# Eight high-half products, then eight low-half products, in a piece of a split-weight matrix product

## The chip, the cores and the metric

One core of one Trainium2 chip runs the whole program. The metric is device time in microseconds, from launch to end; lower is better. The kernel before takes 2523.23 us (median of three runs, 2515.52 to 2528.11).

## What is computed

A decoder trunk of two layers over 256 positions of width 2048. Layer 0 mixes with sliding-window attention and a state-space scan, layer 1 with a recurrent time mixer; each mixer ends in an output projection that is added to x, and each is followed by a squared-ReLU MLP of width 8192. The part that the change touches is the MLP and the two output projections:

```python
def squared_relu_mlp(h, w_up, w_down):
    u = h @ w_up.astype(h.dtype)
    return jnp.square(jax.nn.relu(u)) @ w_down.astype(h.dtype)
...
        x = x + mix.astype(x.dtype)
        h = rms_norm(x, norm_ffn[i])
        x = x + squared_relu_mlp(h, w_up[i], w_down[i]).astype(x.dtype)
```

## The kernel before, in words

Everything is held transposed: 128 channels on the partitions, 256 tokens in the free dimension. A float32 product is made of three products of a shorter format. A weight tile `wt` (128 x 1024, that is eight blocks of 128 x 128) comes in by DMA; ScalarE (ACT) rounds it to `hi` and VectorE (DVE) makes `lo = wt - hi`. The activations are kept the same way, `SA` and `SB`, 16 channel blocks of 512 columns: the first 256 columns are the rounded activations, the other 256 the remainder. For one block TensorE (PE) does `hi` times all 512 columns and `lo` times the first 256. Below, these are called a hi product and a lo product, and the two of one block a pair.

`unit` (line 378) makes one output tile of 128 channels. It goes over two halves h of the 2048 inputs; a half is one tile `wt`, called a piece, with eight pairs. All pairs of a unit add up in one PSUM bank `pu` of 512 columns: the hi product fills the whole bank, the lo product adds to columns 256 to 511. There are two banks `pu` (lines with `pu_119` and `pu_235` in the order below), and three buffers each for `wt`, `hi` and `lo` (126/127, 164/165 and 237/238 for hi/lo).

`mlp` (line 520) runs, four times over: 16 up-units, each followed on ACT and DVE by `eb`, `u`, `uw`, `ut` and the two halves of one block of `SB` (in the second MLP `SA`); then 16 down-units, whose sum is added to x by two DVE adds (`xh<-xh,pu`, later `xT`) before the bank is free again. In the first MLP the last three of the 64 down-units are done elsewhere. `out_proj` (line 1037) is a run of units with the same two adds and, behind them, the next norm's work (`acc`, `SA`). For the first seven tiles of layer 0's output projection the first half is done earlier, so these units have one piece.

The mixers' own projections do not go through `unit`. `feed` (line 431) issues them as three products of 256 columns a block: hi, hi, lo, all into the same 256 columns. That code is not changed. Its rows are called feed below.

In the MLPs and output projections a scheduler sets the order of each engine's instructions by its own estimates; engines then run their queues in that order and wait for semaphores.

Of the kernel before, what the change touches and what calls it, by code (L numbers as in the profile page):

```python
# [295 lines left out]
class Part:  # L296


    def __init__(self, unit, h, src, X=None, n=8, m=P, k0=0, end=16, tiles=None, ready=None, bank=None):
        self.unit, self.key, self.src, self.X, self.n, self.m = unit, unit + (h,), src, X, n, m  # L300
        self.k0, self.end, self.tiles, self.ready, self.bank = k0, end, tiles, ready, bank
# [17 lines left out]
class Trunk:  # L319
# [59 lines left out]
    def unit(self, src, X, h0=0):  # L379
        nc = self.nc  # L380
        ps = self.psu("pu", 2, [P, 512])
        for h in range(h0, 2):
            wt, hi, lo = (self.wp(n, 3, [P, 8 * P], t).rearrange("p (k m) -> p k m", m=P)
                          for n, t in (("wt", F32), ("hi", F32R), ("lo", F32R)))
            nc.sync.dma_start(out=wt, in_=src[:, h * 8:h * 8 + 8, :])
            self.act(hi, wt)
            self.sub(lo, wt, hi.bitcast(F32))
            for kk in range(8):
                k = h * 8 + kk
                self.mm(ps, hi[:, kk, :], X[:, k, :], start=k == 8 * h0, stop=False)  # L390
                self.mm(ps[:, L:], lo[:, kk, :], X[:, k, 0:L], start=False, stop=k == 15)
        return ps

# [661 lines left out]
    def mixer1_in(self, h, SA, SB, scaled, spill, end):  # L1055
# [9 lines left out]
        with tc.tile_pool(name="rh", bufs=1) as rh, tc.tile_pool(name="rht", bufs=1) as rt, \  # L1065
# [10 lines left out]
            def unit(n, j, src, i, m=P, cut=2, bank=None):  # L1076
                s = NK // cut
                return [Part((n, j), q, src[:, q * s:q * s + s, :], (SA, SB)[i not in (0, 3)], s, m, q * s, bank=bank,
                             ready=lambda k: [("mix", i, k)]) for q in range(cut)]

            hidden = [unit("w", 0, ap["w1"], 1, 96), unit("a", 0, ap["a1"], 4, 96),
                      unit("g", 0, ap["g1"][0], 5) + unit("g", 1, ap["g1"][1], 5)]
            parts = [Part(("d", d), q, ap["w_dn0"][3, d][:, q * 8:q * 8 + 8, :], SB, k0=q * 8)
# [665 lines left out]
```

## Time and profile before

| | us |
|---|---|
| median of the runs (3) | 2523.23 |
| lowest, highest | 2515.52, 2528.11 |
| profiled execution, time | 2520.23 |
| profiled execution, span of the trace | 2518.5 |
| PE busy (matmuls) | 2421.8 |
| DVE, ACT, POOL busy | 1768.6, 1315.8, 576.1 |
| granted TensorE clock, mean | 0.983 |

The profiled execution spends 1.7 us outside its span. Units run from about 308 to 1092 us (output projection 0 to 391, MLP 0 behind it) and from about 1754 to the end (output projection 1 to 1802, then MLP 1). In these stretches the granted clock is 1.00. PE's records overlap: the end of a matmul is modelled, so the distance from one start to the next tells the pace, not the duration. In the timeline a row with x2 stands for two instructions of one kind, in turn.

### The profile page before, as it was taken

The numbers are of one execution on the slowest core, as the hardware profiler recorded it, in microseconds if no ns is written. First come the engines' busy times: TensorE is split into PE (matmuls) and PEld (weight loads), VectorE is DVE, ScalarE is ACT, GpSimd is POOL, SyncE is SP. The second block draws the span as 40 slices with busy tenths as digits, with TensorE's granted clock in tenths as the row PEclk, the third lists the DMA queues.
The fourth block names the chain that finished last, engine by engine and source line by source line (L and its number), as shares of the span: only waits on it lengthen the run. The fifth ranks groups of instructions, "written<-read, shape, count | busy, mean of one in ns | idle before, by whom it ended". The sixth has DMA issues, their size and how long they took to land.

```text
span 2518.5 us, 44799 instructions
## 1 busy us (share of the span) xinstructions
PE 2421.8 (96%) x16972; PEld 2165.3 (86%) x16972; DVE 1768.6 (70%) x3330; ACT 1315.8 (52%) x2430; POOL 576.1 (23%) x978
## 2 busy tenths in 40 slices
PE   7999999999999999987998899999999999999999
PEld 7998988888888888877998888888888888888887
DVE  6888776656656656668888888887865665665665
ACT  5455555435435445555555666666653453543543
POOL 3443300000000000036447776774000000000000
PEclk9999999999999999988999899999999999999999
DMA  5333455555555555533544233334555555555554
GB/s 191 139 106 106 142 188 184 187 186 185 187 188 185 185 188 188 201 131 123 175 159 132 84 114 106 112 112 160 186 191 190 188 191 191 188 190 185 187 198 159
DMA packets 130344, 414.67 MB, mean 165 GB/s; under 512 B 23600, under 2 KB 28336, under 8 KB 130128
## 3 DMA queue, kind: packets, MB, share of 16 engines
q1 hardware_dynamic: 128160, 405.91, 47.1%
q0 software_dynamic: 1968, 5.90, 0.6%
q8 instruction: 133, 2.18, 0.3%
q14 instruction: 83, 0.68, 0.1%
HBM read 407.03 MB, written 4.72 MB: 163 GB/s over the span
## 4 chain that ended last, share of the span: by engine, by line
PE 78%; DVE 11%; issue 4%; POOL 3%; ACT 3%; DMA 1%; SPq 0%; POOLq 0%; ACTq 0%; DVEq 0%
PE pu L350 72%; DVE lo L329 2%; PE ps_t L350 1%; PE ps_y L350 1%; POOL xt L329 1%; PE ps_c L350 1%; DVE st L347 1%; ACT hi L326 1%; POOL X L329 1%; PE ps_i L350 1%; PE ps_a L350 1%; DVE AR L329 1%; PE pr L350 0%; PE ps_b L350 0%; ACT ysq L326 0%
## 5 line engine op out<-in xcount | busy, mean ns | idle before, releaser
L329 DVE TENSOR_TENSOR lo<-wt,hi 128x1024 fp32r<-128x1024 f32 (+2 forms) x850 | 898.8, 1060 | 511.7 <-ACT hi L326 494.9
L326 ACT ACTIVATE hi<-wt 128x1024 fp32r<-128x1024 f32 (+2 forms) x945 | 813.6, 873 | 820.3 <-PE pu L350 783.5
L350 PE MATMUL pu<-SA,hi 128*128 128x512 f32 (+2 forms) x4184 | 1154.5, 347 | 10.5 <-ACT SA L326 6.5
L350 PE MATMUL pu<-SB,hi 128*128 128x512 f32 (+2 forms) x3304 | 995.8, 364 | 11.3 <-ACT SB L326 9.2
L350 PE MATMUL pu<-SA,lo 128*128 128x256 f32 (+1 forms) x3168 | 892.1, 282 | 1.5 <-DVE lo L329 1.4
L350 PEld LDWEIGHTS pu<-SA,hi 128*128 128x128 f32 (+1 forms) x4184 | 722.0, 190 | 119.0 <-ACT SA L326 6.5
L350 PE MATMUL pu<-SB,lo 128*128 128x256 f32 x2752 | 773.0, 281 | 0.5 <-DVE lo L329 0.5
L350 PEld LDWEIGHTS pu<-SB,hi 128*128 128x128 f32 (+1 forms) x3304 | 588.1, 190 | 116.5 <-ACT SB L326 10.1
L350 PEld LDWEIGHTS pu<-SA,lo 128*128 128x128 f32 (+1 forms) x3168 | 601.0, 190 | 2.7 <-DVE lo L329 2.1
L350 PEld LDWEIGHTS pu<-SB,lo 128*128 128x128 f32 x2752 | 521.9, 190 | 0.9 <-DVE lo L329 0.7
L1721 POOL DMA_DIRECT2D out<-xT x16 | 8.7, 544 | 699.9 <-DVE xT L329 699.9
L329 POOL TENSOR_TENSOR lo<-wt,hi 128x512 fp32r<-128x512 f32 (+1 forms) x95 | 136.2, 1437 | 127.4 <-ACT hi L326 121.5
L1688 POOL DMA_DIRECT2D xd<-xh x13 | 7.2, 557 | 682.3 <-DVE xh L329 682.3
L329 DVE TENSOR_TENSOR xh<-xh,pu 128x256 f32<-128x256 f32 x164 | 69.1, 421 | 56.5 <-PE pu L350 53.7
L329 DVE TENSOR_TENSOR xT<-xT,pu 128x256 f32<-128x256 f32 x154 | 64.7, 420 | 45.7 <-PE pu L350 43.0
L329 POOL TENSOR_TENSOR xt<-Nb,X 128x60 f32<-128x60 f32 (+14 forms) x240 | 88.4, 368 | 22.9 <-DMA Nb<-dn 6.7
L329 POOL TENSOR_TENSOR X<-X,xt 128x60 f32<-128x60 f32 (+14 forms) x240 | 78.3, 326 | 16.9
L347 DVE SCALAR_TENSOR_TENSOR st<-dx,vec,xh 128x256 f32<-128x256 f32 x80 | 59.9, 763 | 2.9 <-POOL dx L329 2.2
L347 DVE SCALAR_TENSOR_TENSOR uw<-u,rb 128x256 f32<-128x256 f32 x128 | 54.4, 425 | 4.3
L326 ACT ACTIVATE uv<-ps_c,n 64x64 f32<-64x64 f32 x128 | 39.3, 307 | 32.1 <-PE ps_c L350 30.0
L329 DVE TENSOR_TENSOR u<-pu,eb 128x256 f32<-128x256 f32 x128 | 53.4, 417 | 0.0
L326 ACT ACTIVATE ut<-uw 128x256 f32<-128x256 f32 x128 | 51.3, 401 | 2.2 <-DVE uw L347 2.2
(308 smaller groups left out, 2103.2 us busy)
## 6 DMA issues: line engine op xcount, KB each, us to landing
wt<-in_w_up SPq DMA_DIRECT2D x256, 512.0 KB
wt<-in_w_dn SPq DMA_DIRECT2D x256, 512.0 KB
wt<-in_w_in SPq DMA_DIRECT2D x64, 512.0 KB
wt<-in_w_out SPq DMA_DIRECT2D x32, 512.0 KB
wt<-in_w_k SPq DMA_DIRECT2D x32, 512.0 KB
wt<-in_w_v SPq DMA_DIRECT2D x32, 512.0 KB
wt<-in_w_o SPq DMA_DIRECT2D x32, 512.0 KB
wt<-in_w_r SPq DMA_DIRECT2D x26, 512.0 KB
```

What stands on the lines that cost most here:

```text
L326: return self.nc.scalar.activation(out=out, in_=in_, func=func, **kw)
L329: return (eng or self.nc.vector).tensor_tensor(out=out, in0=a, in1=b, op=op)
L347: return self.nc.vector.scalar_tensor_tensor(out=out, in0=a, scalar=s, in1=b, op0=op0, op1=op1)
L350: return self.nc.tensor.matmul(out, lhsT, rhs, start=start, stop=stop)
L1688: spill = lambda d, e=nc.gpsimd: e.dma_start(out=xd[:, d, :], in_=x[d])
L1721: store = lambda d: nc.gpsimd.dma_start(out=ap["out"][:, d, :], in_=x[d])
```

## The change

In each piece, the eight hi products are issued first, then the eight lo products. The same instructions are issued on the same tiles; PSUM accumulation order within a piece changes, and the scheduler sees another program.

```diff
             for kk in range(8):
                 k = h * 8 + kk
                 self.mm(ps, hi[:, kk, :], X[:, k, :], start=k == 8 * h0, stop=False)
+            for kk in range(8):
+                k = h * 8 + kk
                 self.mm(ps[:, L:], lo[:, kk, :], X[:, k, 0:L], start=False, stop=k == 15)
         return ps
```

What it does to the order, at two places. First PE, where the first down-unit of the first MLP follows the last up-unit: before, the end of its second piece (164/165), with the next unit's first products (bank 235, 237/238) behind.

```order
L350 MATMUL pu_119<-SB,hi_164 128x512
L350 MATMUL pu_119<-SB,lo_165 128x256
L350 MATMUL pu_119<-SB,hi_164 128x512
L350 MATMUL pu_119<-SB,lo_165 128x256
L350 MATMUL pu_235<-SB,hi_237 128x512
L350 MATMUL pu_119<-SB,hi_164 128x512
L350 MATMUL pu_119<-SB,lo_165 128x256
L350 MATMUL pu_235<-SB,lo_238 128x256
L350 MATMUL pu_235<-SB,hi_237 128x512
```

The same place after, with the unit's first piece (126/127) ahead of it:

```order
L350 MATMUL pu_119<-SB,hi_126 128x512 x8
L350 MATMUL pu_119<-SB,lo_127 128x256 x8
L350 MATMUL pu_119<-SB,hi_164 128x512 x7
L350 MATMUL pu_235<-SB,hi_237 128x512
L350 MATMUL pu_119<-SB,hi_164 128x512
L350 MATMUL pu_119<-SB,lo_165 128x256 x8
L350 MATMUL pu_235<-SB,hi_237 128x512 x7
L350 MATMUL pu_235<-SB,lo_238 128x256 x8
```

Pairs have become runs of eight. In both programs the scheduler puts the next unit's first hi product ahead of the unit's last one (k = 15); behind that last one stood one lo product of the unit, and now stand eight.

Second DVE, in output projection 0, where units with one piece follow each other: before, the two adds of a unit (`xh<-xh,pu`) stand together.

```order
L329 TENSOR_TENSOR xh<-xh,pu_119 128x256 x2
L329 TENSOR_TENSOR lo_238<-wt_132,hi_237 128x1024
L329 TENSOR_TENSOR acc<-acc,sq 128x256
L347 SCALAR_TENSOR_TENSOR SA<-xh,vec,SA 128x256
L329 TENSOR_TENSOR xh<-xh,pu_235 128x256 x2
L329 TENSOR_TENSOR lo_127<-wt_120,hi_126 128x1024
L329 TENSOR_TENSOR acc<-acc,sq 128x256
L347 SCALAR_TENSOR_TENSOR SA<-xh,vec,SA 128x256
```

After, at the same place:

```order
L329 TENSOR_TENSOR xh<-xh,pu_119 128x256
L329 TENSOR_TENSOR lo_238<-wt_132,hi_237 128x1024
L329 TENSOR_TENSOR acc<-acc,sq 128x256
L347 SCALAR_TENSOR_TENSOR SA<-xh,vec,SA 128x256
L329 TENSOR_TENSOR xh<-xh,pu_119 128x256
L329 TENSOR_TENSOR xh<-xh,pu_235 128x256
L329 TENSOR_TENSOR lo_127<-wt_120,hi_126 128x1024
L329 TENSOR_TENSOR acc<-acc,sq 128x256
```

Between the two adds of a unit there now stand a `lo` and the norm's work of the unit before; the down-units have a `lo` between their two adds in the same way. ACT's order moves the same way (a `hi` one place forward) in output projection 0 and in the last down-units of the first MLP; POOL's and the DMA queue's orders stay as they were.

## Rows read from the trace of the kernel before

**Rows 1.** The page: PE's busy time, and ACT's hi (mean ns, idle before, releaser).

```profile
PE 2421.8 (96%) x16972; PEld 2165.3 (86%) x16972; DVE 1768.6 (70%) x3330; ACT 1315.8 (52%) x2430; POOL 576.1 (23%) x978
...
L326 ACT ACTIVATE hi<-wt 128x1024 fp32r<-128x1024 f32 (+2 forms) x945 | 813.6, 873 | 820.3 <-PE pu L350 783.5
```

**Rows 2.** Groups by line and form, PE: hi products of 512 columns.

```profile
L350 PE MATMUL pu<-SB,hi 128*128 128x512 f32 x2200 | 773.4, 397 | 0.0
...
L350 PE MATMUL pu<-SA,hi 128*128 128x512 f32 x2152 | 757.6, 397 | 1.0 <-DVE xT L329 1.0
```

**Rows 3.** Windows of 90 us: busy us and count by engine, clock, DMA share.

```profile
397.00:487.00 90.00, 90.00 (x510) 77.89 (x509) 57.19 (x81) 49.34 (x80) 0.00 (x0) 1.00 0.54 186
1808.00:1898.00 90.00, 90.00 (x520) 78.50 (x519) 57.90 (x83) 50.44 (x81) 0.00 (x0) 1.00 0.54 188
```

**Rows 4.** Timeline (start, length, instruction), PE and weight loads, at 1000 us.

```profile
1000.18 0.40 PE L350 MATMUL pu<-SA,hi 128*128 128x512 f32 x1
1000.19 0.19 PEld L350 LDWEIGHTS pu<-SA,lo 128*128 128x128 f32 x1
1000.41 0.28 PE L350 MATMUL pu<-SA,lo 128*128 128x256 f32 x1
1000.42 0.19 PEld L350 LDWEIGHTS pu<-SA,hi 128*128 128x128 f32 x1
...
1001.24 0.40 PE L350 MATMUL pu<-SA,hi 128*128 128x512 f32 x1
```

**Rows 5.** Timeline, PE: two ends of the quicker stretch, and its pairs.

```profile
1765.43 0.47 PE L350 MATMUL pu<-SA,hi 128*128 128x512 f32 x1 [1.04 <-DVE xT L329]
...
1899.87 0.39 PE L350 MATMUL pu<-SA,hi 128*128 128x512 f32 x1
...
1901.95 0.39 PE L350 MATMUL pu<-SA,hi 128*128 128x512 f32 x1
...
2246.45 0.86 PE L350 MATMUL pu<-SA,hi 128*128 128x512 f32 x2
```

**Rows 6.** Timeline, PE, at 52 us: feed, products of 256 columns.

```profile
52.08 0.28 PE L350 MATMUL pu<-SA,lo 128*128 128x256 f32 x1
52.20 0.40 PE L350 MATMUL pu<-SA,hi 128*128 128x256 f32 x2
52.44 0.28 PE L350 MATMUL pu<-SA,lo 128*128 128x256 f32 x1
```

**Rows 7.** Timeline, PE, at 11 us: weights of 16 columns, products of 256.

```profile
11.44 0.28 PE L350 MATMUL pu<-SA,lo 128*16 128x256 f32 x1
11.45 0.09 PEld L350 LDWEIGHTS pu<-SA,hi 128*16 128x16 f32 x1
11.56 0.28 PE L350 MATMUL pu<-SA,hi 128*16 128x256 f32 x1
```

**Rows 8.** Timeline, all engines, first down-unit of the first MLP, second piece.

```profile
478.81 0.40 PE L350 MATMUL pu<-SB,hi 128*128 128x512 f32 x1
...
478.89 1.06 ACT L326 ACTIVATE hi<-wt 128x1024 fp32r<-128x1024 f32 x1 [1.50 <-PE pu L350]
...
479.99 1.23 DVE L329 TENSOR_TENSOR lo<-wt,hi 128x1024 fp32r<-128x1024 f32 x1 [0.81 <-ACT hi L326]
...
481.13 0.42 DVE L329 TENSOR_TENSOR SB<-ut,SB 128x256 fp32r<-128x256 f32 x1
...
481.60 0.19 PEld L350 LDWEIGHTS pu<-SB,hi 128*128 128x128 f32 x1 [0.25 <-DVE SB L329]
481.94 0.40 PE L350 MATMUL pu<-SB,lo 128*128 128x256 f32 x2
...
482.18 0.40 PE L350 MATMUL pu<-SB,hi 128*128 128x512 f32 x1
```

**Rows 9.** Timeline, DVE, output projection 0: adds of two units.

```profile
322.82 0.87 DVE L329 TENSOR_TENSOR xh<-xh,pu 128x256 f32<-128x256 f32 x2
...
325.66 0.86 DVE L329 TENSOR_TENSOR xh<-xh,pu 128x256 f32<-128x256 f32 x2
```

## The prediction

> **What bounds the kernel now.** I read the page first, then the groups by form, windows of equal length, and the timeline. PE is busy for 96% of the span, and ACT spends 783.5 us waiting in front of `hi` for PE to give a buffer back [rows 1]: in the units the split of the weights waits for PE, not PE for the split. The windows of the MLPs say the same: PE 90.00 of 90, DVE 57, ACT 49, the DMA engines 54% busy, clock 1.00 [rows 3]. So here the time is the number of products times the pace at which PE starts them, plus the few places where a product waits for its operands. The change leaves the number alone. There are 2200 + 2152 = 4352 pairs [rows 2]; 1 ns on a pair is 4.35 us, or 0.17%.
>
> The pace is read from starts, since durations overlap. In one stretch three pairs take 1001.24 - 1000.18 = 1.06 us, 353.3 ns a pair: 0.23 to 0.24 us from a hi product to the lo product behind it, 0.11 to 0.12 from lo to hi [rows 4]. In another stretch six pairs take 1901.95 - 1899.87 = 2.08 us, 346.7 ns [rows 5]. Both have the full clock, and the windows show the same two paces: 510 and 520 products in 90 us [rows 3]. The quicker one runs from 1765.43 to 2246.45, and each end is a place where PE had just waited [rows 5]. 481 us at 346.7 ns are about 1,380 pairs; the other 2,970 run at 353.3. Mean: (1380 x 346.7 + 2970 x 353.3) / 4350 = 351.2 ns. The stream of products thus has two paces 2% apart, and which one holds changes where PE is stopped. The change gives it a new rhythm, and that is what matters most here.
>
> **The change, part by part.** *Weight loads.* Each product has its own load, before and after. A load starts 0.01 us behind the product ahead of it [rows 4], so it has that product's time to finish. Before, eight loads of a piece lie behind hi products and eight behind lo products; after, it is still eight and eight. Loads behind 256-column products occur throughout feed, 0.12 us a product (0.36 us for three) [rows 6]. With weights of only 16 columns the distance is 0.12 us too [rows 7], so the load's size hardly shows.
>
> *Lo behind lo.* The price is on record: 0.12 us in feed [rows 6], and 0.12 between the two lo products that follow each other at the unit boundary (481.94, next hi 482.18, two distances) [rows 8]. I take 119 ns, against a mean of about 117 in pairs.
>
> *Hi behind hi, without a wait.* No row shows it. From above, the longest distance behind a hi product is 0.24 us [rows 4]; from below, 227 ns, from fitting columns and products: feed has 768 columns in three products in 360 ns [rows 6], the quicker stretch 768 in two products in 346.7 [rows 5]; the difference, 13.3 ns, would be the fixed part of a product, and a hi product would cost (346.7 - 2 x 13.3) x 512/768 + 13.3 = 226.7 ns. I take 231, the quicker stretch's share for a hi product (346.7 less some 116), because a run of equal products has no alternation for the three-pair rhythm (1.06 us) of the slower stretch to come from. A pair then costs 231 + 119 = 350 ns, 1.2 below the mean: **-5.2 us**. Bounds: 226.7 + 120 = 346.7 gives -19.6; 241 + 120 = 361 gives +42.6.
>
> *From up-units to down-units, eight times.* The first down-unit needs the last block of `SB`. Its remainder is written at 481.13 for 0.42 us and the load behind it starts at 481.60. From 478.81 to 482.18, PE does nine pairs, 3.18 us at 353.3 ns, in 3.37: 0.19 us lost now [rows 8]. After, seven hi products and the next unit's first stand ahead of the last hi, whose load is wanted at 478.81 + 7 x 0.231 = 480.43 instead of about 481.3. But the chain to `SB` is itself held up by a `hi` on ACT at 478.89 that waited 1.50 us for PE, and a `lo` on DVE at 479.99 behind it [rows 8]. PE's last read of a `hi` buffer comes eight lo products earlier, 0.94 us; the `lo` buffer comes free where it did, at the end of the piece. So the `lo` can start at about 479.1, `SB` is ready at 480.7, and the load is 0.32 us late where it was 0.19: +0.13 us, eight times, **+1.1 us**. If the chain gains nothing, the load still comes at 481.60, 1.17 us late: +7.8. If the wait goes, -1.5.
>
> *The adds.* In output projection 0, seven units have one piece, and DVE does 2.84 us of work for each (325.66 - 322.82) [rows 9] against eight pairs, 2.83 us, on PE. With the second add behind `lo`, `acc` and `SA`, a bank comes free about 2.84 us behind its last product instead of 0.9, and with two banks PE wants it after 2.83. I take 0.1 us a unit, **+0.7**, bounds 0 and 2.5. In the down-units the bank is given back one `lo` (1.23 us) later, but is wanted only 16 pairs, 5.65 us, later: nothing, and nothing as long as that `lo` isn't late by another 3 us.
>
> *At no cost.* ACT's `hi` may start 0.94 us earlier, but ACT was waiting for PE anyway. `wt` comes free when DVE has made `lo`, which follows the `lo` buffer, so the transfers keep their times. `lo` is needed 8 x 0.23 = 1.85 us later than `hi`, which would end a PE wait for `lo`; PE is at 90.00 of 90 in the MLPs [rows 3], so there is no such wait to win. Feed is unchanged.
>
> Sum: -5.2 + 1.1 + 0.7 = -3.4 us. The profiled execution took 2520.2 (span 2518.5 plus 1.7 outside), which becomes 2516.8; it stands 3.0 below the median of 2523.2, which becomes 2519.8.
>
> **The rivals.** *Quicker: the regular pace.* Feed's products of one width keep one distance, 0.12, 0.24, 0.36 [rows 6]. If runs of hi products lock in the same way at the fitted 226.7 ns, every pair costs 346.7: -19.6 + 1.8 = -17.8, or **2505**. For it: the fit meets both feed and the quicker stretch. Against: 227 is below every distance that I read behind a hi product.
>
> *Slower: lo runs paced by their weight loads.* Behind a 256-column product a load of 128 columns has little room. If lo behind lo stays at feed's full 120 ns while hi keeps the slower stretch's 236 (353.3 less 117), a pair costs 356: +20.9 + 1.8, or **2546**. It decides from 353.6 ns a pair on: (353.6 - 351.2) x 4.35 + 1.8 is +12, the half per cent. For it: the slower pace is the commoner one, and feed is the nearest row to a run of lo products. Against: it takes the worse end of both. If the load took its whole record of 0.19 us [rows 4], a lo run would cost 73 ns more a product, some 280 us; feed, with such loads at 0.12, excludes it.
>
> The Trainium skill (TensorE: Matmul & The Clock Gate, section LDWEIGHTS (loading the stationary operand)) puts a load at columns / 1.2 ns, 107 ns for 128 columns. By that, an estimate, a load just fits behind a 256-column product, and this change, which puts a load of that length behind each lo product as the old order did, would cost nothing; the 0.12 us of feed agree that it fits, the 0.12 us with 16-column weights show that it isn't the bound.
>
> *Slower: the wait for `SB`.* +7.8 and +2.5 with the pace unchanged: **2534**, within half a per cent.
>
> That the order isn't what the diff says is excluded by the rows of the order above.
>
> **How the numbers follow.** A difference of over 0.5%, about what a measurement here can tell from none, is 12.6 us: below 2510.6 or above 2535.8. Forecast, 348 to 353.5 ns a pair (2511 to 2535): 0.42. Regular pace, 2505: 0.33. Load-paced lo runs, 2546: 0.20. The wait for `SB`, 2534: 0.05, of which a fifth beyond the bound. Faster 0.33, same 0.45, slower 0.22 with the tail of the forecast. The range takes in 2505 with 2 us for a better fixed part, and 2546: 2503 to 2546; what is outside is a pair under 346 or over 356.
>
> **What would show it.** Starts in a hi run (0.23 here; 0.227 for the quicker rival; 0.236 for the slower) and in a lo run (0.119); products in a 90 us window of MLP 0 (514 here, 519, 506); load late at the eight places by 0.3 us or by 1.2; in output projection 0, first hi products waiting for DVE. The forecast is wrong if the hi runs don't stand between 229 and 235 ns, whatever the total says.

## The result, and the profile after

The changed kernel takes 2534.87 us (median of 17 runs, 2531.66 to 2539.92) against 2521.97 before (17 runs, 2514.05 to 2529.34): 1.0055 times as long, 95% interval 1.0045 to 1.0066. So it is some 13 us slower, where the prediction's sum gave 2519.8, a little faster than before. The total lies inside the stated range of 2503 to 2546, but it moved the other way. The profiled execution took 2534.19 us, of which its span is 2532.4.

First the page, answering to [rows 1]:

```profile
PE 2422.9 (96%) x16972; PEld 2178.4 (86%) x16972; DVE 1747.3 (69%) x3330; ACT 1312.5 (52%) x2430; POOL 570.8 (23%) x978
...
L326 ACT ACTIVATE hi<-wt 128x1024 fp32r<-128x1024 f32 (+2 forms) x945 | 811.7, 873 | 802.1 <-PE pu L350 768.5
```

Then the groups by form, answering to [rows 2] (name, shape, count, busy us and mean ns, idle before and its releaser):

```profile
L350 PE MATMUL pu<-SB,hi 128*128 128x512 f32 x2200 | 555.1, 394 | 12.8 <-DVE xh L329 12.8
L350 PE MATMUL pu<-SA,hi 128*128 128x512 f32 x2152 | 540.6, 393 | 2.7 <-DVE xT L329 2.1 <-ACT hi L326 0.2
```

The page's totals hardly differ from before. The groups' busy time does, 555.1 where it was 773.4 for `SB`, but it counts overlapping records once, and in a run of eight they overlap each other; the mean of one record, 394 ns, is almost that of before, 397. What is new is small: before, the hi products on `SB` never waited; now they wait 12.8 us for `xh` on DVE. The list of PE's waits says in how many pieces (us in total, times, longest):

```profile
PE pu L350 <- DVE xh L329: 12.8, 8, 2.4
```

Before, that list had no such row. `xh` is written by the adds of a down-unit, so eight times PE stood at a unit's first product until an add gave a `pu` bank back. Windows show the place. Each row is a stretch: busy us and count of PE, weight loads, DVE, ACT and POOL, then clock, DMA share and GB/s. The first answers to [rows 3]; the second is in the last down-units of the first MLP.

```profile
397.00:487.00 90.00, 90.00 (x517) 78.97 (x517) 56.64 (x80) 49.27 (x77) 0.00 (x0) 1.00 0.53 187
1020.00:1080.00 60.00, 50.87 (x277) 43.80 (x276) 27.49 (x42) 22.70 (x32) 4.32 (x8) 0.97 0.48 159
```

Before, the same sixty microseconds read:

```profile
1020.00:1080.00 60.00, 60.00 (x341) 51.89 (x340) 38.49 (x55) 31.80 (x44) 5.58 (x10) 1.00 0.61 208
```

In an up-stretch of MLP 0 there are more products than before, 517 against 510. In the last down-units there are 277 against 341. The table below lays the profiled executions side by side, from start to start of the products named, in us. The two right-hand columns are experiments that are told further down.

| stretch | before | after | scale late | scale late, `w_o` pairs |
|---|---|---|---|---|
| start to first 512-column product | 314.07 | 311.89 | 311.52 | 315.79 |
| output projection 0, to `exb` of MLP 0 | 82.32 | 82.30 | 82.29 | 82.31 |
| MLP 0, to its last 512-column product | 696.18 | 705.04 | 687.33 | 687.34 |
| to the first `pr` product | 27.77 | 29.72 | 28.60 | 28.60 |
| mixer 1, to the first `w_o` product of 512 columns | 638.24 | 640.34 | 638.31 | 640.46 |
| output projection 1, to `exb` of MLP 1 | 49.08 | 52.26 | 52.26 | 49.06 |
| MLP 1, to the last product | 705.13 | 705.18 | 705.15 | 705.16 |

MLP 0 lost 8.9 us and output projection 1 lost 3.2. MLP 1, with as many grouped units, lost nothing. The first stretch and mixer 1 hold code that no edit touches, and move by 2 to 4 us among these four profiles; over all nine, mixer 1 takes 636.9 to 644.9. One thing in the table is bookkeeping: behind the last 512-column product of MLP 0 stand eight `lo` products in a grouped kernel and one in pairs, so seven of them, 0.83 us, move from the row of MLP 0 to the next. That is the whole step from 27.77 to 28.60.

**The pace** is one of the things that went as forecast. Timeline of PE (start, length, instruction, count), to be held against [rows 4]:

```profile
1001.49 2.00 PE L350 MATMUL pu<-SA,hi 128*128 128x512 f32 x8
1003.33 1.11 PE L350 MATMUL pu<-SA,lo 128*128 128x256 f32 x8
1004.28 0.63 PE L350 MATMUL pu<-SA,hi 128*128 128x512 f32 x2
```

Eight `hi` take 1003.33 - 1001.49 = 1.84 us, 230 ns each; eight `lo` take 0.95, 119 each: 349 ns a pair.

**The stop.** One round of the last down-units, timeline of all engines (in brackets: idle before, and what ended it):

```profile
1044.39 1.23 DVE L329 TENSOR_TENSOR lo<-wt,hi 128x1024 fp32r<-128x1024 f32 x1 [3.78 <-ACT hi L326]
1045.53 0.42 DVE L329 TENSOR_TENSOR xh<-xh,pu 128x256 f32<-128x256 f32 x1
...
1045.98 0.42 ACT L326 ACTIVATE sq<-xh 128x256 f32<-128x256 f32 x1 [0.68 <-DVE xh L329]
...
1046.10 2.08 PE L350 MATMUL pu<-SB,hi 128*128 128x512 f32 x8 [1.34 <-DVE xh L329]
1046.24 0.54 POOL L1690 DMA_DIRECT2D xd<-xh  x1 [6.60 <-DVE xh L329]
...
1051.01 0.51 ACT L326 ACTIVATE xh<-xh,vec 128x256 f32<-128x256 f32 x1 [4.61 <-DMA xd<-xh]
1051.42 1.99 ACT L326 ACTIVATE hi<-wt 128x1024 fp32r<-128x1024 f32 x2
...
1052.50 1.23 DVE L329 TENSOR_TENSOR lo<-wt,hi 128x1024 fp32r<-128x1024 f32 x1 [4.75 <-ACT hi L326]
1053.64 0.41 DVE L329 TENSOR_TENSOR xh<-xh,pu 128x256 f32<-128x256 f32 x1
...
1054.20 2.08 PE L350 MATMUL pu<-SB,hi 128*128 128x512 f32 x8 [2.28 <-DVE xh L329]
1054.35 0.54 POOL L1690 DMA_DIRECT2D xd<-xh  x1 [7.57 <-DVE xh L329]
```

It is a ring. POOL issues the spill of block d to `xd` (1046.24). The in-place scaling of the same block, `xh<-xh,vec`, may not overwrite `xh` until that transfer has read it, and waits on ACT until 1051.01: 4.77 us. Both next `hi` stand behind it (1051.42), the `lo` on DVE waits for its `hi` (1052.50), and the second add of the unit stands behind this `lo` (1053.64). That add gives PE its bank and lets the next spill go (1054.35). One round is 4.77 + 0.41 + 1.08 + 1.14 + 0.71 = 8.11 us, where sixteen pairs take 5.59.

In the source the scaling of block d stands two units later, in `f0(d + 2)`. But the scheduler that orders each engine's instructions had moved it up into the round of its own block, before the change as after it. Before, ACT's order was square, `hi`, scaling, `hi`:

```profile
1048.82 0.42 ACT L326 ACTIVATE sq<-xh 128x256 f32<-128x256 f32 x1
...
1049.08 0.54 POOL L1688 DMA_DIRECT2D xd<-xh  x1 [5.11 <-DVE xh L329]
...
1050.61 1.06 ACT L326 ACTIVATE hi<-wt 128x1024 fp32r<-128x1024 f32 x1 [1.38 <-PE pu L350]
...
1053.58 0.51 ACT L326 ACTIVATE xh<-xh,vec 128x256 f32<-128x256 f32 x1 [1.90 <-DMA xd<-xh]
1053.99 1.04 ACT L326 ACTIVATE hi<-wt 128x1024 fp32r<-128x1024 f32 x1
```

From the spill's issue to the scaling it was 4.50 us there too, but one `hi` had been done in the meantime, and PE was fed. After, with that `hi` moved ahead of the square, the order is square, scaling, `hi`, `hi`.

### The profile page after: what moved, and what is told of

Read it like the earlier page. It is cut to its first block, busy times and chain, and to the rows that moved or that the text cites. A ratio compares the mean times of both kernels' runs of the same rounds, so it can differ in the third digit from the quotient of the medians.

```text
span 2532.4 us, 44806 instructions
## 1 busy us (share of the span) xinstructions
PE 2422.9 (96%) x16972; PEld 2178.4 (86%) x16972; DVE 1747.3 (69%) x3330; ACT 1312.5 (52%) x2430; POOL 570.8 (23%) x978
## 4 chain that ended last, share of the span: by engine, by line
PE 74%; DVE 11%; issue 6%; POOL 4%; ACT 3%; DMA 2%; SPq 0%; POOLq 0%; DVEq 0%; ACTq 0%
PE pu L350 68%; DVE lo L329 2%; PE ps_t L350 1%; DVE st L347 1%; ACT hi L326 1%; PE ps_y L350 1%; POOL xt L329 1%; PE ps_c L350 1%; DMA xd<-xh 1%; POOL X L329 1%; PE ps_a L350 1%; DVE AR L329 1%; PE ps_i L350 1%; PE pr L350 1%; DMA wt<-in_w_r 0%
## 5 line engine op out<-in xcount | busy, mean ns | idle before, releaser
L350 PE MATMUL pu<-SA,hi 128*128 128x512 f32 (+2 forms) x4184 | 937.6, 345 | 13.0 <-ACT SA L326 7.1
L350 PE MATMUL pu<-SB,hi 128*128 128x512 f32 (+2 forms) x3304 | 779.6, 363 | 25.1 <-DVE xh L329 12.8
L350 PEld LDWEIGHTS pu<-SA,hi 128*128 128x128 f32 (+1 forms) x4184 | 703.8, 190 | 94.1 <-ACT SA L326 8.2
L350 PEld LDWEIGHTS pu<-SB,hi 128*128 128x128 f32 (+1 forms) x3304 | 573.4, 192 | 103.0 <-ACT hi L326 14.1
L350 PE MATMUL pu<-SA,lo 128*128 128x256 f32 (+1 forms) x3168 | 590.5, 283 | 1.4 <-DVE lo L329 1.4
L350 PEld LDWEIGHTS pu<-SA,lo 128*128 128x128 f32 (+1 forms) x3168 | 488.4, 191 | 23.4 <-DVE lo L329 1.8
L350 PE MATMUL pu<-SB,lo 128*128 128x256 f32 x2752 | 467.2, 284 | 1.4 <-DVE lo L329 1.4
L350 PEld LDWEIGHTS pu<-SB,lo 128*128 128x128 f32 x2752 | 409.6, 192 | 23.3 <-DVE lo L329 1.8
```

The costliest lines, as they stand in the source:

```text
L350: return self.nc.tensor.matmul(out, lhsT, rhs, start=start, stop=stop)
```

## The experiments

Four kernels ask whether this order on ACT is the cause, or the grouped products themselves; three more ask what the grouped order is worth without it. By the source the last round of the first MLP has thirteen down-units (16 less the three done elsewhere), of 282 units that the change regroups; the expectations count fourteen, and 156. In the diffs, `run` is how many `hi` products stand in a row before their `lo` products (1 is the order before, 8 the change).

**Pairs in the last down-units alone.**

```
-                    ps = self.unit(ap[f"w_dn{l}"][c, d], U)
+                    ps = self.unit(ap[f"w_dn{l}"][c, d], U, run=1 if (l, c) == (0, 3) else 8)
```

> The grouped order everywhere, but pairs (one `hi`, one `lo`) in the fourteen last down-units of the first MLP (stage 0, c = 3). Theory (the loss sits in these units, where `scale` waits on ACT for the spill's transfer ahead of both next `hi`s): the 14 us of stops of the changed kernel's profile are gone and the one pace of 349.1 ns stays elsewhere, so 2521 us (2518 to 2524) against 2535 for the change, level with the kernel before. Rival A (the loss is spread over all grouped units, in bank returns and late `lo`s): only the 14 grouped units of 156 change, about 2534. ACT's order in these units should read hi, sq, hi, scale as before the change.

Measured: 2516.43 us, 0.9981 of before (0.9972 to 0.9989; before 2521.79). MLP 0 took 688.80 us. ACT's timeline in the last down-units:

```profile
1035.58 0.51 ACT L326 ACTIVATE xh<-xh,vec 128x256 f32<-128x256 f32 x1 [2.31 <-DMA xd<-xh]
1036.00 1.04 ACT L326 ACTIVATE hi<-wt 128x1024 fp32r<-128x1024 f32 x1
1036.95 0.40 ACT L326 ACTIVATE sq<-xh 128x256 f32<-128x256 f32 x1
1037.87 1.06 ACT L326 ACTIVATE hi<-wt 128x1024 fp32r<-128x1024 f32 x1 [0.52 <-PE pu L350]
```

The scaling still waits, 2.31 us here, but one `hi` has gone ahead of it and one stands behind, and PE does not stop (60.00 of 60 us busy from 1020 to 1080). The loss is in these thirteen units. More: with them mended the grouped order is a little faster than the pairs, and the time lies below the expected 2518 to 2524.

**Grouped in the last down-units alone.**

```
-    def unit(self, src, X, h0=0, run=8):
+    def unit(self, src, X, h0=0, run=1):
...
-                    ps = self.unit(ap[f"w_dn{l}"][c, d], U)
+                    ps = self.unit(ap[f"w_dn{l}"][c, d], U, run=8 if (l, c) == (0, 3) else 1)
```

> Pairs everywhere as before, the eight `hi` and eight `lo` products grouped in the fourteen last down-units of the first MLP alone. Theory: the whole loss is here, 2522 + 14 = 2536 us (2532 to 2539), with stops of 1.5 to 2.7 us between a `lo` and the next unit's first `hi`, eight or more of them. Rival A (loss spread over all grouped units): 2522 + a tenth of 13 = 2523.

Measured: 2540.04 us (5 runs), 1.0071 (1.0058 to 1.0083), somewhat more than expected. PE's waits:

```profile
PE pu L350 <- DVE xh L329: 11.9, 6, 3.2
```

Thirteen of the 282 units lose 18 us, more than the 13 of the whole change, which gains some pace elsewhere.

**Grouped everywhere, the scaling held back.** Nothing of the products is touched; on ACT, the scaling of block d - 2 may not be placed ahead of the square of block d. (`fx` now returns that square.)

```
-                    fx(d)
+                    s = fx(d)
                     spill(d)
                     if d >= 2:
-                        scale(d - 2)
+                        with tc.issue_after(s.ins):
+                            scale(d - 2)
```

> The grouped order everywhere as in the change; only the in-place scaling of block d on ACT is held behind the square of block d + 2, so it comes after its spill has long landed and no `hi` stands behind a waiting `scale`. Theory: PE's stops in the last down-units go, 2521 us (2518 to 2524), or a few us less if the mixer's start gains too. Rival B (the stops come of the grouped order itself: the bank goes back one `lo` of 1.23 us later and the second add stands behind it on DVE, whoever is ahead of the `hi`s on ACT): 2532 to 2536, as the change.

Measured: 2515.05 us, 0.9978 (0.9969 to 0.9987), again below the expected 2518 to 2524. A window, then rows of ACT and DVE from the timeline of all engines:

```profile
1020.00:1080.00 60.00, 60.00 (x347) 52.87 (x346) 36.76 (x55) 31.00 (x45) 7.22 (x12) 1.00 0.65 212
```

```profile
1040.69 0.40 ACT L326 ACTIVATE sq<-xh 128x256 f32<-128x256 f32 x1
...
1041.00 0.50 ACT L326 ACTIVATE xh<-xh,vec 128x256 f32<-128x256 f32 x1
...
1043.42 0.42 DVE L329 TENSOR_TENSOR xh<-xh,pu 128x256 f32<-128x256 f32 x1 [1.04 <-PE pu L350]
1043.76 1.22 DVE L329 TENSOR_TENSOR lo<-wt,hi 128x1024 fp32r<-128x1024 f32 x1
...
1044.90 0.41 DVE L329 TENSOR_TENSOR xh<-xh,pu 128x256 f32<-128x256 f32 x1
```

The scaling has no wait left, and PE has 347 products in the window (before 341, change 277). The `lo` still stands between the two adds and the bank still comes back one `lo` later. That costs nothing, because the `lo` is not late. So the rival that blamed the grouped order itself falls.

**Pairs, with ACT's order of the change.** The scaling goes right behind its square, and the `hi` of later units are held behind it.

```
-            self.act(hi, wt)
+            if len(self.held) > 1:
+                with self.tc.issue_after(self.held[-2]):
+                    self.act(hi, wt)
+            else:
+                self.act(hi, wt)
...
-                    if d >= 2:
-                        scale(d - 2)
+                    if d < end - 2:
+                        self.held.append(scale(d).ins)
```

> The kernel before with its pairs; only ACT's order in the last down-units of the first MLP is held as the change has it: square of block d, scaling of block d, then both `hi`s of the unit after next. Theory: the scaling's wait for the spill holds both `hi`s without any grouping, 2536 us (2530 to 2540), PE stops of 1.5 to 2.7 us in these units. Rival B (it takes the grouped products to lose the time): 2522 to 2524, as before.

Measured: 2552.87 us (4 runs), 1.0125 (1.0111 to 1.0139): twice the expected loss, with no grouped product in the kernel. From the timeline:

```profile
1042.82 0.51 ACT L326 ACTIVATE xh<-xh,vec 128x256 f32<-128x256 f32 x1 [4.98 <-DMA xd<-xh]
...
1043.24 1.99 ACT L326 ACTIVATE hi<-wt 128x1024 fp32r<-128x1024 f32 x2
...
1044.33 0.49 PE L350 MATMUL pu<-SB,hi 128*128 128x512 f32 x1 [0.18 <-ACT hi L326]
...
1045.59 0.39 PE L350 MATMUL pu<-SB,lo 128*128 128x256 f32 x1 [0.77 <-DVE lo L329]
```

The order on ACT is the cause. Part of the extra loss shows what grouping is good for: a pair needs the `lo` at its first step, so each late unit stops a second time for the `lo`, 1.26 us from start to start (1044.33 to 1045.59) where 0.23 is usual. There are ten such stops, some 10 us. A run of eight `hi` would have had work for 1.84 us. In this profile MLP 0 lost 23.4 us in all. Mixer 1 and MLP 1, whose code the edit leaves alone, were another 6.4 and 3.3 longer: MLP 1 for a larger share of the pairs' slower pace (from 2100 us on, where the kernel before had it from 2246 on), mixer 1 for a cause that was not found.

**Pairs, the scaling held back.** The edit of the third experiment in the kernel before.

> The kernel before with its pairs; only the in-place scaling of block d is held behind the square of block d + 2 on ACT, as in the run with the grouped order. It tells whose the gain of that run is (2515.05 against 2521.79 us). Theory (the gain is the grouped order's one pace of 349.1 ns a pair, and the late scaling only takes away the stops that the change brought): 2520 to 2523 us here, since before's `scale` never stopped PE. Rival C (before's own waits of ACT for the spill, 8.0 us in nine waits, cost time too and the late scaling wins it): about 2515, and the grouped order is worth nothing by itself.

Measured: 2523.5 us, 1.0004 (0.9984 to 1.0024; before 2523.82). Holding the scaling back by itself changes nothing that can be measured here, so the 0.2% of the grouped kernel come from the products' order. The stretch says it more sharply than the totals, whose intervals just touch: MLP 0 took 696.16 us here, 696.18 before and 687.33 in the third experiment.

This kernel also shows the two paces of the pairs. Here is one of its windows, then the same one of the kernel before:

```profile
1900.00:2050.00 150.00, 150.00 (x851) 130.04 (x850) 90.23 (x118) 68.62 (x91) 0.00 (x0) 1.00 0.58 186
```

```profile
1900.00:2050.00 150.00, 150.00 (x868) 131.18 (x867) 91.79 (x120) 69.79 (x92) 0.00 (x0) 1.00 0.54 190
```

The products of MLP 1 have the same order in both kernels, yet one runs at 868 products in 150 us and the other at 851. MLP 1 took 705.13 us in the one and 711.85 in the other. In the second and fourth experiments the pairs of MLP 0 ran at the quick pace from about 484 to 839 us, where the kernel before had the slow one throughout. The order of the products alone thus does not settle which pace a stretch of pairs gets. That it differs between executions of one kernel is likely but not shown, as each kernel has one profile. The spread of the runs fits in part: among the runs of the last three experiments the kernels in pairs spread over 21 us (29 runs of before, 2509 to 2531) and 20 us (12 here), the sixth and seventh over 6 and 9 (12 each). Among those of the first four, before spread over 9 us (21 runs) and the third, grouped, over 8 (11 runs).

**Output projection 1 in pairs.** The third experiment with one more edit:

```
-            ps = self.unit(w[d], Y, h0=1 if d < early else 0)
+            ps = self.unit(w[d], Y, h0=1 if d < early else 0, run=8 if part is None else 1)
```

> Grouped order with the late scaling, and pairs in output projection 1 alone. From the first `w_o` product of 512 columns to the `exb` products of MLP 1 the grouped kernels took 52.26, 51.67 and 52.26 us and the pair kernels 49.08, 49.06 and 48.57. Theory (there a `lo` on DVE stands behind the adds to `xT` and the grouped unit gives its bank back late): 49 us in that stretch, 2512 us in all. Rival D (the difference belongs to what the earlier stages leave in the queues): still 52 us and 2515.

Measured: 2513.3 us, 0.9967 (0.9951 to 0.9982). The stretch took 49.06 us, as expected. The total's interval overlaps that of the third experiment, so the total alone does not tell the two apart; the stretch does. Why the grouped order loses there is read from the third experiment's timeline, DVE and then PE:

```profile
1762.17 1.22 DVE L329 TENSOR_TENSOR lo<-wt,hi 128x1024 fp32r<-128x1024 f32 x1
1763.30 0.42 DVE L329 TENSOR_TENSOR acc<-acc,sq 128x256 f32<-128x256 f32 x1
1763.64 0.48 DVE L347 SCALAR_TENSOR_TENSOR SB<-xT,vec,SB 128x256 fp32r<-128x256 f32 x1
1764.03 0.41 DVE L329 TENSOR_TENSOR xT<-xT,pu 128x256 f32<-128x256 f32 x1
...
1767.15 0.41 DVE L329 TENSOR_TENSOR xT<-xT,pu 128x256 f32<-128x256 f32 x1
```

```profile
1766.52 1.11 PE L350 MATMUL pu<-SA,lo 128*128 128x256 f32 x8
1767.70 2.06 PE L350 MATMUL pu<-SA,hi 128*128 128x512 f32 x8
```

These units have one piece. The second add stands behind `lo`, `acc` and `SB`, so the bank comes back at 1767.56 and the unit that wants it starts at 1767.70 instead of about 1767.47 (one `lo` distance behind the last `lo`). Such a stop of 0.24 us comes at every second unit, four times, and once one of 0.37; the product behind each is 0.08 us late too. That is 1.7 us of the 3.2. Another 1.1 us is a single wait for `xT`, 2.1 us long and 1.0 in the pair kernel. And the pairs ran this stretch at their quick pace: 2.5 ns on 104 pairs are 0.3 us.

**Runs of two and of four.** The third experiment's kernel with `run=2` in MLP 0 and `run=4` in MLP 1.

> Late scaling; MLP 0 in runs of two `hi` and two `lo` products, MLP 1 in runs of four and four, output projections in runs of eight. It asks how the pace depends on the length of a run: pairs showed two paces, 346.7 and 353.3 ns, runs of eight one of 349.1. If the pace is a sum of switches (a `hi` behind a `lo`, a `lo` behind a `hi`) and steady steps, runs of two and four lie between 349 and 351 and the time is 2515 to 2519 us; if runs of two or four lock as pairs do, a stretch at about 347 or 353 shows again.

Measured: 2517.43 us, 0.998 (0.9966 to 0.9994). Two windows, MLP 0 and MLP 1:

```profile
500.00:650.00 150.00, 150.00 (x863) 130.90 (x862) 90.93 (x121) 71.44 (x97) 0.00 (x0) 1.00 0.59 189
1900.00:2050.00 150.00, 150.00 (x857) 131.10 (x856) 88.67 (x117) 69.04 (x91) 0.00 (x0) 1.00 0.58 187
```

MLP 0 took 686.44 us (687.33 in eights) and MLP 1 took 707.99 (705.15). The pace by starts: in twos 160 pairs take from 500.26 to 556.00, 348.3 ns a pair, where eights take 349.2; in fours 160 pairs take from 1900.54 to 1956.68, 350.8 ns, and from 2101.37 to 2157.37, 350.0. The total came as expected, but the sum of switches and steady steps falls: with eights at 349.2 and fours at some 350.4 it would put twos near 353. No stretch near 353 shows, nor one at 347, though the fours have two levels of their own. The length of a run matters little once there is one, and eights may stay.

## Why the prediction was wrong

*The pace: right.* Hi runs stand at 230 ns in the mean (231 taken; single distances are 226 to 236), lo runs at 119 (119 taken), 349 a pair (350 taken). MLP 0 has 517 products in its window (514 forecast). What the pace gives back shows once the stops are gone: MLP 0 takes 687.33 us instead of 696.18, of which 8.0 us are real and 0.8 is the bookkeeping of the table. MLP 1 gains nothing (705.13 and 705.15), because in the profile of before 62% of it had the quick pace already [rows 5], a mean of 0.62 x 346.7 + 0.38 x 353.3 = 349.2 ns. Output projection 0 gains nothing either; late first products, told below, eat most of the 0.8 us. The two rivals on the pace fall: neither 227 and 120 nor 236 and 120 is there. The prediction's own test, hi runs between 229 and 235 ns, came out as it asked, and the total still went the wrong way: the test looked at the pace alone.

*The mean of before: true of one profile only.* The 351.2 ns came from one execution's two stretches. In the fifth experiment's profile MLP 1, with the same order of products, has another share of each pace and takes 6.7 us longer, so the gain over a mean pair was known to a few microseconds at best.

*From up-units to down-units: about right.* Answering to [rows 8], in the changed kernel:

```profile
475.99 1.23 DVE L329 TENSOR_TENSOR lo<-wt,hi 128x1024 fp32r<-128x1024 f32 x1 [0.77 <-ACT hi L326]
...
477.13 0.42 DVE L329 TENSOR_TENSOR SB<-ut,SB 128x256 fp32r<-128x256 f32 x1
477.60 0.19 PEld L350 LDWEIGHTS pu<-SB,hi 128*128 128x128 f32 x1 [0.38 <-DVE SB L329]
```

The load waited 0.38 us for `SB`, which the chain reached sooner, as argued. Products start 341 and 338 ns apart there where 226 and 227 are usual, 0.23 us lost where 0.19 was before: +0.3 us in eight places, against +1.1. The rival of a 1.17 us wait falls. Its 2534 is the number nearest to the measured 2534.87, but by luck: its cause is not there.

*The adds: the wrong place.* In output projection 0, two first products of a unit are late, which costs 0.25 us each with the slower product behind: 0.5 us against +0.7. But output projection 1, which has thirteen units of one piece, was not costed at all, and there the grouped order loses 3.2 us ([rows 9] show the same adds in the other projection).

*The down-units: the step that failed.* It read "nothing, and nothing as long as that `lo` isn't late by another 3 us". The condition was right, and the third experiment shows the "nothing". But in the last down-units of the first MLP the `lo` is late: it follows a `hi` that stands behind a scaling that waits for a DMA, and DVE waits 3.6 to 5.4 us for that `hi` at the eight stops. There products start 1.05 to 2.67 us apart; beyond the usual 0.12 that is 14.0 us, and the product behind each stop is 0.08 late too, 0.6 us. On top, the clock fell:

```profile
1062.90:1066.40 3.50, 3.50 (x13) 2.99 (x12) 0.91 (x3) 0.00 (x0) 0.00 (x0) 0.51 0.91 294
1093.70:1097.10 3.40, 3.40 (x11) 2.76 (x11) 2.18 (x5) 0.33 (x1) 0.19 (x1) 0.50 0.88 296
```

In these two places, each behind four of the stops, the granted clock is 0.51 and 0.50, the lower level of 1.2 GHz. Hi products start 427 ns apart instead of 230, and lo products 213 instead of 119: some 1.55 us each time, 3.1 in both. The three parts, 14.0, 0.6 and 3.1, are all that MLP 0 lost against the third experiment, 705.04 - 687.33 = 17.7 us. One more stop of PE, for a `lo` at 1104.55 right behind MLP 0, costs 1.0 us and makes most of the step from 28.60 to 29.72. With the pace's -8.0, output projection 1's +3.2 and 1.1 for that step the sum is +14.0 us, where the two profiled spans differ by 13.9 (the untouched stretches, -2.2 and +2.1, cancel) and the medians by 12.9.

The warning was in the trace of before. The list of ACT's waits there has this row for the last down-units (us in total, times, longest):

```profile
ACT xh L326 <- DMA xd<-xh: 8.0, 9, 1.9
```

ACT was already waiting for the spill nine times, up to 1.9 us, with one `hi` ahead of the wait and one behind, and PE did not feel it. The order of the change showed one `hi` moving to the other side. The prediction costed the new order of PE and DVE in these units, but not that of ACT, where only the wait of `hi` for PE was read [rows 1]; its line that ACT "was waiting for PE anyway" does not hold here. In the changed kernel the same row reads:

```profile
ACT xh L326 <- DMA xd<-xh: 42.2, 11, 5.3
```

*At no cost: right outside these units.* In the up-units and the first three rounds of down-units, which have no scaling, no `hi`, `wt` or `lo` holds PE. MLP 1's last down-units store their blocks too but have no in-place scaling, and they lose nothing: from 2436 to 2520 PE is busy 84.00 of 84 us.

One thing stays open. What decides whether a stretch of pairs runs at 346.7 or 353.3 ns was not found. Inside the MLPs the switches stand where up-units pass to down-units and PE briefly waits, but at most of these places the pace stays as it was; no more is shown.

## What to carry to other kernels

Where a scheduler sets the order, a change on one engine can move instructions on another. There, look for an instruction that waits for a DMA and count what stands behind it before and after: a wait that hid behind one buffer of lead stops everything when two stand behind it. An in-place operation on a buffer that is being stored is such a wait, and here it cost nothing to place it two units later. And once a fix for the side effect is found, run the idea again with it: here the grouped order turned from 0.5% slower to 0.2% faster than the pairs, 0.3% with output projection 1 left in pairs (the last step is shown by that stretch, not by the totals).

## What the hardware showed beside that

The alternating stream of 512- and 256-column products does not keep one pace. With the same order of products a stretch runs at 346.7 or at 353.3 ns a pair at full clock, and the two profiles compared above differ by 6.7 us in one MLP for it. Grouped, the spread was smaller in these profiles: 348.3 ns by twos, 350.0 and 350.8 by fours, 349.2 by eights. And in one phase four short stops of PE, 7 us in sum, were twice followed by the lower clock level, a granted clock of 0.51 from 1062.90 to 1066.40 and of 0.50 from 1093.70 to 1097.10.
